# Opening of a two-layer hybrid backbone, ordered anew: filter tables first, modulation and the first wide matmuls in quarters, three units open

## The chip, the cores and the metric

The kernel runs on one NeuronCore of one Trainium2 chip. A core has five engines that work through their own instruction queues in order and wait for one another through semaphores: TensorE (PE) multiplies matrices, VectorE (DVE) and ScalarE (ACT) work elementwise, GpSimd (POOL) has next to nothing to do here, and SyncE (SP) issues the DMAs. The metric is device time in microseconds (us) of one execution.

## What is computed

A flow-matching backbone of two layers over 256 latent tokens and 256 context tokens of width 1024, all in float32. Each layer is a half-step SwiGLU, a token mixer and another half-step SwiGLU; shift, scale and gate of every sub-layer come from a modulation of the conditioning vectors. Layer 0 mixes with differential attention, layer 1 with a Hyena long convolution. What the change touches, cut from the reference:

```python
def modulation(cond, w, b):
    m = jax.nn.silu(cond) @ w + b
    return jnp.split(m[..., None, :], N_MOD, axis=-1)

def swiglu(h, wi, wo):
    a, u = jnp.split(h @ wi, 2, axis=-1)
    return (jax.nn.silu(a) * u) @ wo

def half_ffn(x, shift, scale, gate, wi, wo, g, b, alpha):
    y = swiglu(x * (1.0 + scale) + shift, wi, wo)
    return layer_norm(alpha * x + 0.5 * gate * y, g, b)

def hyena_filters(n, w1, b1, f1, w2, b2, f2, w3):   # z: 33 position features of n = 256 positions
    h = jnp.sin(f1 * (z @ w1 + b1))
    h = jnp.sin(f2 * (h @ w2 + b2))
    h = (h @ w3) * jnp.exp(-t * deltas)
    return h[:, :D_MODEL], h[:, D_MODEL:]
```

The two Hyena filters are later needed as spectra. Neither they nor the first modulation depend on the tokens, so the kernel computes them in its opening, beside the first SwiGLU.

## The kernel before

**Arithmetic.** Float32 products are made of rounded halves: a value is cast to a high half on ACT (`wH`, `xh`, `hhe`), the rest is the low half on DVE (`wL`, `xl`, `hle`), and three matmuls (high x high, high x low, low x high) replace one.

**The first SwiGLU** ("wide") takes latent and context tokens together: 512 columns. Its 22 *units* are 128 columns of the hidden width; a unit is two accumulations, `pa` and `pu`, over 8 tiles of the contraction, so 48 matmuls with 512 columns. Its weights are one 1 MB DMA (`raw<-wia`), split by `Stream._split` (L237, L238) into one of three slots (`W_BUFS`).

**The opening** is written out by hand. `START` is the order of the loads on SP's queue; `ORDER` is a list of words that `run` (L648) records one after the other, and within it every engine keeps that order (`tc.manual_schedule`). What follows it is ordered by a scheduler. The words:

- `n1`, `n2`: the two small layers of the filter net, `filter_net` (L555) with `sine` (L541: six steps on DVE, then ACT's Sin). The output is `hid1`, `hid2`.
- `t`*dt*: `filter_taps` (L575), for half d of the channels and half t of the positions: two matmuls of 64 rows (`hp`), forward and backward filter, times a decay table (`hh`).
- `ah`: split of the table of the transform. `v`*dt*: sum and difference of forward and backward taps (`heo`, L591), each split in halves.
- `s`*df*: one spectrum tile, six matmuls (`hsp`, L334) and a copy of the result by ACT (`hsb`, L607). `S`: the spectra are stored.
- `a`: `ada_unit` (L449) multiplies one 1 MB piece of the modulation weights (`rawa<-adx`) with the conditioning, four matmuls in four column strips of 32 into one psum tile (`adaps`). `F`: `ada_end` (L460) copies it (ACT, L463), transposes it (PE, `adat`) and sums it on DVE to shift and scale. `p`: `scales` (L621) adds 1 to the scale.
- `x`*j*: `modulated` (L630) scales token tile j (DVE, L633, two halves), casts the high half (ACT, L636), and leaves the low half (DVE, L628) to the next `x` or to `xl`.
- `W`: the next weights are split. `u`: `wide_unit` (L641) opens a unit and runs contraction tiles 0 to 3 of it; `g`*n* runs tiles 4 to 7 of the n-th open unit.
- `k`*n*: n filler matmuls (`warm`), which compute nothing.

Before, the modulation comes in two halves of four pieces each: `F` after the fourth and the eighth. The first half of the token tiles (`x0` to `x3`) is scaled after the first `F`, the second half after the other. Two units are opened.

**SP's queue** is strict in the opening: a load that finds no free buffer (three for `rawa`, two for `raw`) holds back all that stand behind it. A DMA also waits for the one eight places ahead of it, whose semaphore it uses again.

Of the kernel before, what the change touches and what calls it, by code (L numbers as in the profile page):

```python
# [13 lines left out]
AF = mybir.ActivationFunctionType  # L14
# [48 lines left out]
ADA_FFN = dict(b0=[2 * f for f in range(1, 9)], a1=[3 * f for f in range(1, 4)], b1=[])  # L63


START = """ah d0 a00 a01 a02 fw3 a03 w0 d2 z0 a10 z1 z2 z3 a11 d1 a12 w1 d3 a13 z4 z5 z6 z7 w2 cb""".split()

ORDER = """n1 k18 n2 k18 S a k3 t00 a ah a a W F p0 k4 t01 x0 x1 x2 x3 xl v00 k1 v01 k3 a t11 u0 a a W s01 s00
s02 a F p1 x4 x5 t10 x6 s04 x7 s03 xl u1 g0 v10 v11 g1 s10 s13 s14 s12 s11 S""".split()

RAWA_BUFS = 3
RAW_BUFS = 2
# [65 lines left out]
def lay_out(x):  # L142
    f32 = np.float32
    con = shape_constants()
    a = {}

    def put(name, arr):
        a[name] = np.ascontiguousarray(arr, dtype=f32)

    def tcols(m):  # L150
        return m.reshape(m.shape[0], KT, P).transpose(2, 1, 0)

    put("xc", np.concatenate([tcols(x["x"][0]), tcols(x["ctx"][0])], axis=2).transpose(1, 0, 2))
# [12 lines left out]
    cols(V_CB, x["hy_conv_b"][0])  # L166
    cols(V_DS, x["hy_d_skip"][0])
    cols(V_SG, x["da_subln_g"][0])
    vec[:, V_LAM:V_LAM + 256] = np.broadcast_to(x["da_lambda"].reshape(1, 256), (P, 256))
    put("cb", np.broadcast_to(np.concatenate([x["c"].reshape(D), x["c_ctx"].reshape(D)]), (P, 2 * D)))  # L170
    for i, k in enumerate(("hy_fb1", "hy_ff1", "hy_fb2", "hy_ff2")):
        vec[:64, V_F + i] = x[k][0]
    put("vec", vec)

    zf = np.zeros((64, 384), f32)
    zf[:33, 0:256] = con["z"]
    zf[:33, 256:320] = x["hy_fw1"][0]
    zf[:, 320:384] = x["hy_fw2"][0]
    put("zf", zf)
    put("fw3", x["hy_fw3"][0])  # L180
    for k in ("rope", "decay", "a_u", "a_h", "b_i", "ident"):
        put(k, con[k].reshape(P, -1))

    for i in range(2):
        w = x["ada_w"][i].reshape(KT, P, 9 * D)
        if i == 0:
            put("adx0", w[:, :, :2048].reshape(4, 2, P, 2, 2, 512).transpose(4, 0, 2, 1, 3, 5))
# [12 lines left out]
    put("who", x["hy_w_o"][0].reshape(KT, P, 4, 2, P).transpose(2, 1, 3, 0, 4))  # L200
    return a
# [108 lines left out]
def backbone(ctx, tc, A, out):  # L310
# [59 lines left out]
    for what in START:  # L370
        if what == "cb":
            items.append(dict(kind="d", src=A["cb"], dst=lambda: condb.rearrange("p q k -> p (q k)")))
        elif what[0] == "d":
            q = int(what[1])
            tload(decay, A["decay"][:, 512 * q:512 * q + 512], "tabf")
        elif what == "fw3":
            table(fw3, "tabf", A["fw3"], range(0, 2049, 512), 64)
        elif what == "ah":
            table(a_h, "tabf", A["a_h"], A_H)
        elif what[0] == "z":  # L380
            zload(int(what[1:]))
# [61 lines left out]
    mod = [cp.tile([P, 2, 72], F32, name=f"mod{i}") for i in range(2)]  # L443


    ada_first = [(h, k) for h in (0, 1) for k in range(4)]
    ada_ps = {}

    def ada_unit():  # L449

        h, k = ada_first.pop(0)
        it = st.get("a")
        if k == 0:
            ada_ps[h] = adap.tile([P, 512], F32, name="adaps", tag="ada")
        for j in range(4):
            nc.tensor.matmul(ada_ps[h][32 * j:32 * j + 32, :], condS[:, 2 * k + j // 2, :],
                             it["raw"][:, 512 * j:512 * j + 512], start=k == 0, stop=True, skip_group_check=True)
        st.done(it)

    def ada_end():  # L460
        h, ps = ada_ps.popitem()
        sb = blk("adasb")
        S.copy(sb, ps)  # L463
        pt = adap.tile([P, 512], F32, name="adat", tag="ada")
        for b in range(4):
            nc.tensor.transpose(pt[:, P * b:P * b + P], sb[:, P * b:P * b + P], ident)
        v = pt.rearrange("p (b j s) -> p s j b", b=4, j=4)

        def cols3(t, o):
            return t[:, o:o + 16].rearrange("p (j h b) -> p j h b", j=2, h=2)[:, :, h, :]  # L470

        for q in range(2):
            m3 = cols3(mod[0][:, q, :], 0)
            V.tensor_tensor(m3, v[:, q, 0:2, :], cols3(vec, V_ADAB), OP.add)
            V.tensor_tensor(m3, v[:, q, 2:4, :], m3, OP.add)

    def ada_side(n, later=ADV):

# [60 lines left out]
    C1, C2, C3 = split_2pi()  # L539

    def sine(dst, ps, bcol, fcol):  # L541
        a = blk("sa")[:64, :T]
        n = blk("sn")[:64, :T]
        V.tensor_scalar(a, ps, vec[:64, bcol:bcol + 1], vec[:64, fcol:fcol + 1], OP.add, OP.mult)
# [4 lines left out]
        V.tensor_scalar(a, a, PI_LO, -PI_LO, OP.min, OP.max)  # L549
        S.activation(dst, a, AF.Sin)  # L550
# [2 lines left out]
    ah = []  # L553

    def filter_net(n):  # L555
        ps = bank("hp")
        if n == 0:
            mm(ps[:64, :T], zf[:33, 256:320], zf[:33, 0:256], True, True)
        else:
            mm(ps[:64, :T], zf[:64, 320:384], hid[0][:64, :T], True, True)  # L560
        sine(hid[n][:64, :T], ps[:64, :T], V_F + 2 * n, V_F + 2 * n + 1)

    def table_split():
        for n, t in enumerate(a_h):
# [8 lines left out]
    raw_taps = {}  # L573

    def filter_taps(dh, tt):  # L575
        hs = []
        for g in range(2):
            ph = bank("hp3")
            mm(ph, hid[1][:64, P * tt:P * tt + P], fw3[2 * g + dh][:64, :], True, True)
            hh = blk("hh")  # L580
            V.tensor_tensor(hh, ph, decay[2 * dh + tt], OP.mult)
            if g == 1 and tt == 0:
                V.memset(hh[0:1, :], 0.0)
            hs.append(hh)
        raw_taps[dh, tt] = hs
# [32 lines left out]
    X = []  # L618
    late = []

    def scales(half):  # L621
        hs = slice(4 * half, 4 * half + 4)
        V.tensor_scalar(s1[:, :, hs], mod[0][:, :, 8 + 4 * half:12 + 4 * half], 1.0, None, OP.add)
# [24 lines left out]
    def run(what):  # L648
# [187 lines left out]
    def ffn_wide():  # L836
        nrm = Norm(Z, 512)
        for half in range(2):
# [618 lines left out]
```

## Time and profile before

| what | value |
|---|---|
| time, median of 3 runs (lowest, highest) | 1357.56 us (1355.3, 1360.0) |
| profiled execution: time, span | 1356.75 us, 1355.0 us |
| busy PE, DVE, ACT | 1310.6, 1035.4, 660.5 us |
| mean granted clock of PE | 0.975 |
| moved by DMA | 261.38 MB, mean 193 GB/s |

The profile is of one execution. In its rows, `pa<-xh,wH` names what is written and what is read, without buffer numbers; L634 or the like is the line in the kernel, and matmuls of all kinds are recorded in one helper line (L334 before). A wait in brackets names who ended it. PE's ends are modelled: matmuls follow one another faster than their durations say. A float32 matmul that isn't split shows as two PE instructions.

### The profile page before, as it was taken

What the parts mean: (1) busy time and instruction counts of PE and PEld (TensorE: products, weight loads), DVE (VectorE), ACT (ScalarE), POOL (GpSimd) and SP (SyncE); (2) the same over time, 40 slices, a digit from 0 to 9 for tenths busy, and PEclk for the clock granted to TensorE, in tenths of its full rate; (3) what the DMA queues carried; (4) which work ended last, traced back from release to release, by engine and by line L of the source; (5) the groups of instructions that cost most, each with busy time, mean ns of one, the idle gap of its engine ahead of it and who ended that gap; (6) DMA issues with size and microseconds to landing.
All of it is one profiled execution on the core that took longest, in us unless ns stands there. A gap on an engine that the chain in (4) does not pass through costs nothing.

```text
span 1355.0 us, 19282 instructions
## 1 busy us (share of the span) xinstructions
PE 1310.6 (97%) x7424; PEld 1127.2 (83%) x7424; DVE 1035.4 (76%) x1921; ACT 660.5 (49%) x1177; POOL 12.7 (1%) x12
## 2 busy tenths in 40 slices
PE   7999999999999999998999999999999999999997
PEld 4688888888888888887888888888899889888886
DVE  3899988789886777778776668766668789766664
ACT  1443322232233866665755447655446444666543
POOL 0000000000000000000000000000000110000000
PEclk8999999999998999998999998999999989899998
DMA  9967788888942212121655463654664434355452
GB/s 290 395 238 260 274 328 335 335 333 316 321 163 78 94 63 94 63 94 63 215 189 178 154 215 138 218 186 158 217 205 150 143 125 157 132 183 194 157 190 76
DMA packets 44418, 261.38 MB, mean 193 GB/s; under 512 B 4964, under 2 KB 6692, under 8 KB 19624
## 3 DMA queue, kind: packets, MB, share of 16 engines
q1 hardware_dynamic: 44328, 260.16, 53.7%
q8 instruction: 58, 0.95, 0.3%
q14 instruction: 32, 0.26, 0.1%
HBM read 256.99 MB, written 3.15 MB: 192 GB/s over the span
## 4 chain that ended last, share of the span: by engine, by line
PE 87%; DVE 7%; ACT 3%; DMA 1%; issue 1%; ACTq 0%; SPq 0%
PE py L334 24%; PE pa L334 23%; PE pu L334 23%; PE pxv L334 5%; PE pv L334 2%; DVE wL L238 2%; ACT wH L237 1%; PE hsp L334 1%; PE pka L334 1%; PE pkb L334 1%; PE warm L334 1%; PE uf L334 1%; PE lnst L334 1%; DMA raw<-wia 1%; PE po L334 1%
## 5 line engine op out<-in xcount | busy, mean ns | idle before, releaser
L238 DVE TENSOR_TENSOR wL<-raw,wH 128x1024 fp32r<-128x1024 f32 (+1 forms) x356 | 388.1, 1108 | 111.7 <-ACT wH L237 108.9
L237 ACT CAST wH<-raw 128x1024 fp32r<-128x1024 f32 (+1 forms) x356 | 329.0, 956 | 212.9 <-PE py L334 97.1
L334 PE MATMUL pa<-xhl,wH 128*128 128x512 f32 x520 | 188.7, 400 | 5.6 <-DVE xhl L813 5.6
L334 PE MATMUL pu<-xhl,wH 128*128 128x512 f32 x520 | 188.0, 398 | 0.0
L334 PE MATMUL py<-g,wH 128*128 128x512 f32 (+1 forms) x594 | 186.6, 372 | 0.0
L489 DVE SCALAR_TENSOR_TENSOR rawa<-rawa,condb 128x1024 f32<-128x1024 f32 x128 | 151.5, 1220 | 1.4 <-DMA rawa<-adr 1.1
L334 PE MATMUL py<-g,wL 128*128 128x256 f32 x528 | 147.8, 280 | 0.0
L334 PE MATMUL pa<-xhl,wL 128*128 128x256 f32 x520 | 146.6, 282 | 0.0
L334 PE MATMUL pu<-xhl,wL 128*128 128x256 f32 x520 | 146.3, 281 | 0.0
L334 PEld LDWEIGHTS py<-g,wH 128*128 128x128 f32 x594 | 107.2, 188 | 21.0
L334 PEld LDWEIGHTS pa<-xhl,wH 128*128 128x128 f32 x520 | 98.7, 190 | 29.4 <-DVE xhl L813 4.2
L334 PEld LDWEIGHTS pu<-xhl,wH 128*128 128x128 f32 x520 | 98.9, 190 | 23.3
L334 PEld LDWEIGHTS py<-g,wL 128*128 128x128 f32 x528 | 99.6, 189 | 0.1
L334 PEld LDWEIGHTS pa<-xhl,wL 128*128 128x128 f32 x520 | 99.5, 191 | 0.1
L334 PEld LDWEIGHTS pu<-xhl,wL 128*128 128x128 f32 x520 | 99.3, 191 | 0.0
L843 ACT ACTIVATE sil<-pa 128x512 f32<-128x512 f32 x22 | 13.2, 599 | 152.7 <-PE pa L334 152.7
L334 PE MATMUL pxv<-xhl,wH 128*128 128x256 f32 x384 | 73.1, 292 | 1.3 <-ACT xhl L811 1.1
L334 PE MATMUL pa<-xh,wH 128*128 128x512 f32 x176 | 68.6, 390 | 0.0
L334 PE MATMUL pa<-xh,wL 128*128 128x512 f32 x176 | 68.5, 389 | 0.0
L334 PE MATMUL pu<-xl,wH 128*128 128x512 f32 x176 | 68.5, 389 | 0.0
L334 PE MATMUL pa<-xl,wH 128*128 128x512 f32 x176 | 68.5, 389 | 0.0
L334 PE MATMUL pu<-xh,wL 128*128 128x512 f32 x176 | 68.5, 389 | 0.0
(314 smaller groups left out, 2601.8 us busy)
## 6 DMA issues: line engine op xcount, KB each, us to landing
rawa<-adr SPq DMA_DIRECT2D x64, 1024.0 KB, 7.1
raw<-wia SPq DMA_DIRECT2D x44, 1024.0 KB, 4.8
raw<-wib SPq DMA_DIRECT2D x44, 1024.0 KB, 4.8
raw<-woa SPq DMA_DIRECT2D x32, 704.0 KB, 4.2
raw<-wob SPq DMA_DIRECT2D x32, 704.0 KB, 4.1
rawa<-adx SPq DMA_DIRECT2D x8, 1024.0 KB, 9.4
raw<-wqk SPq DMA_DIRECT2D x8, 1024.0 KB, 4.8
raw<-whv SPq DMA_DIRECT2D x8, 1024.0 KB, 4.8
```

The lines of the kernel that those rows point to most:

```text
L237: nc.scalar.copy(h[:, d], it["raw"][:, s:e])
L238: nc.vector.tensor_tensor(lo[:, d], it["raw"][:, s:e], h[:, d].bitcast(F32), OP.subtract)
L334: return nc.tensor.matmul(o, l, r, start=start, stop=stop, skip_group_check=True)
L489: V.scalar_tensor_tensor(junk if q else w, w, 1.0, condb[:, q, :], OP.mult, OP.mult, accum_out=mod[i][:, q, 2 * u + h:2 * u + h + 1])
L843: S.activation(s, pa, AF.Silu)
```

## The change

- **Loads.** The filter's output weights, which were four 64-row loads, are laid out as two of 128 rows, with the forward filter on rows 0 to 63 and the backward on rows 64 to 127; the first half, two decay tables and the transform's table come first. The modulation pieces are cut differently: a quarter of the columns needs two pieces instead of half of them four.
- **Taps on both row halves.** The second filter layer writes its 64 outputs twice, on 128 partitions, and the two matmuls of `t` use different halves of PE's rows.
- **Quarters.** `F`*h* comes after every second `a`, four times in all, and is followed by the scaling of two token tiles. `g`*nh* runs two contraction tiles of open unit n; `o` opens a unit without running anything. Three units are open.
- **Scaling on ACT.** `modulated` does both halves with an ACT activation (L644 after) instead of DVE's.
- **Fillers.** 72 instructions of the first two `k` become 40; there are `k6`, `k8` and `k10` before the first wide matmul, and none after it.

The core of the diff:

```diff
-START = """ah d0 a00 a01 a02 fw3 a03 w0 d2 z0 a10 z1 z2 z3 a11 d1 a12 w1 d3 a13 z4 z5 z6 z7 w2 cb""".split()
+START = """f0 d0 d2 ah a00 a01 w0 z0 z1 a10 a11 z2 z3 w1 f1 d1 d3 a20 a21 z4 z5 w2 a30 a31 z6 z7 cb""".split()
...
-ORDER = """n1 k18 n2 k18 S a k3 t00 a ah a a W F p0 k4 t01 x0 x1 x2 x3 xl v00 k1 v01 k3 a t11 u0 a a W s01 s00
-s02 a F p1 x4 x5 t10 x6 s04 x7 s03 xl u1 g0 v10 v11 g1 s10 s13 s14 s12 s11 S""".split()
+ORDER = """n1 k10 n2 k10 ah t00 t01 a a k6 v00 F0 k8 p0 W x0 x1 xl k10 v01 o g00 s00 s01 a s02 a s03 F1 p1 s04 x2 x3 xl
+g01 W t10 t11 o g10 v10 g11 v11 a a s10 F2 p2 s11 x4 x5 xl g02 g12 s12 s13 W s14 o g20 g21 a a F3 p3 g22 x6 x7 xl
+g03 g13 g23 S""".split()
...
-    ada_first = [(h, k) for h in (0, 1) for k in range(4)]
+    ada_first = [(h, k) for h in range(4) for k in (0, 1)]
...
-            nc.tensor.matmul(ada_ps[h][32 * j:32 * j + 32, :], condS[:, 2 * k + j // 2, :],
+            nc.tensor.matmul(ada_ps[h][32 * j:32 * j + 32, :], condS[:, 4 * k + j, :],
...
         for q in range(2):
-            m3 = cols3(mod[0][:, q, :], 0)
-            V.tensor_tensor(m3, v[:, q, 0:2, :], cols3(vec, V_ADAB), OP.add)
-            V.tensor_tensor(m3, v[:, q, 2:4, :], m3, OP.add)
+            m3 = cols(mod[0][:, q, :], 0)
+            V.tensor_reduce(m3, v[:, q], AX.X, OP.add)
+            V.tensor_tensor(m3, m3, cols(vec, V_ADAB), OP.add)
...
         for g in range(2):
             ph = bank("hp3")
-            mm(ph, hid[1][:64, P * tt:P * tt + P], fw3[2 * g + dh][:64, :], True, True)
+            r = slice(64 * g, 64 * g + 64)
+            nc.tensor.matmul(ph, hid[1][r, P * tt:P * tt + P], fw3[dh][r, :], start=True, stop=True,
+                             skip_group_check=True, tile_position=(64 * g, 0))
...
         for q in range(2):
-            V.tensor_scalar(hv[:, T * q:T * q + T], Z[j][:, T * q:T * q + T], s1[:, q, j:j + 1],
-                            mcol(0, q, 0, j), OP.mult, OP.add)
+            S.activation(hv[:, T * q:T * q + T], Z[j][:, T * q:T * q + T], AF.Identity, bias=mcol(0, q, 0, j),
+                         scale=s1[:, q, j:j + 1])
...
-        elif a == "u":
+        elif a == "o":
             opened.append(wide_unit())
-            gemm(opened[-1][3], X, KT, 0, 4)
         elif a == "g":
-            gemm(opened[int(b)][3], X, KT, 4)
+            gemm(opened[int(b)][3], X, KT, 2 * int(c), 2 * int(c) + 2)
```

Where the change moves instructions, in three places. First ACT's queue around the second modulation result. Before, from the weights of the second unit on (`hsb` copies a spectrum, `adasb` the modulation, `xh` is the cast of a scaled token tile):

```order
L237 CAST wH_421<-raw_264 128x1024 x2
L607 COPY hsb_436<-hsp_429 128x512
L607 COPY hsb_445<-hsp_438 128x512
L607 COPY hsb_454<-hsp_447 128x512
L463 COPY adasb_462<-adaps_357 128x512
L636 CAST xh_477<-hv_474 128x512
L237 CAST wH_683<-raw_372 128x1024
L636 CAST xh_483<-hv_480 128x512
```

After, from the second of the first five spectra on:

```order
L619 COPY hsb_353<-hsp_346 128x512
L619 COPY hsb_375<-hsp_368 128x512
L619 COPY hsb_390<-hsp_383 128x512
L468 COPY adasb_392<-adaps_355 128x512
L619 COPY hsb_411<-hsp_404 128x512
L644 ACTIVATE hv_413<-z_222,mod0_128,s1_133 128x256 x2
L647 CAST xh_416<-hv_413 128x512
L644 ACTIVATE hv_419<-z_224,mod0_128,s1_133 128x256 x2
L647 CAST xh_422<-hv_419 128x512
L239 CAST wH_439<-raw_226 128x1024 x2
```

The scaling (`hv`) now stands on ACT itself, behind the copy of a fifth spectrum, and the next unit's weights stand behind it.

Second, PE's queue at the same place. Before, behind the last piece of the modulation:

```order
L456 MATMUL adaps_357<-rawa_362,condS_122 32x512 x4
L466 MATMUL adat_464<-ident_86,adasb_462 128x128 x4
L334 MATMUL hp3_487<-tabf_106,hid2_130 128x512
L334 MATMUL hp3_491<-tabf_110,hid2_130 128x512
L334 MATMUL hsp_503<-hhe_329,ahh_242 128x512
L334 MATMUL hsp_503<-hle_330,ahh_242 128x512
```

After, from the end of spectrum s03 to the first matmuls of the third token tile:

```order
L336 MATMUL hsp_383<-hhe_319,ahl_195 128x512
L471 MATMUL adat_394<-ident_86,adasb_392 128x128 x4
L336 MATMUL hsp_404<-hhe_249,ahh_190 128x512
L336 MATMUL hsp_404<-hle_250,ahh_190 128x512
L336 MATMUL hsp_404<-hhe_249,ahl_191 128x512
L336 MATMUL hsp_404<-hhe_313,ahh_194 128x512
L336 MATMUL hsp_404<-hle_314,ahh_194 128x512
L336 MATMUL hsp_404<-hhe_313,ahl_195 128x512
L336 MATMUL pa_323<-xh_416,wH_280 128x512
L336 MATMUL pa_323<-xl_417,wH_280 128x512
```

Between the transposition and the matmuls that need its result, PE now has one spectrum; before, it had taps, two spectra and half a unit of wide matmuls.

Third, DVE's queue at the last modulation result. Before (`heo` and `hle` are the even and odd taps):

```order
L474 TENSOR_TENSOR mod0_126<-adat_464,vec_84 128x2x4
L475 TENSOR_TENSOR mod0_126<-adat_464,mod0_126 128x2x4
L474 TENSOR_TENSOR mod0_126<-adat_464,vec_84 128x2x4
L475 TENSOR_TENSOR mod0_126<-adat_464,mod0_126 128x2x4
L623 TENSOR_SCALAR s1_131<-mod0_126 128x2x4
L633 TENSOR_SCALAR hv_474<-z_364,s1_131,mod0_126 128x256 x2
```

After, at the fourth quarter (`junk<-rawa,condb` is a side product for a later modulation):

```order
L479 TENSOR_REDUCE mod0_128<-adat_676 128x2x2
L480 TENSOR_TENSOR mod0_128<-mod0_128,vec_84 128x2x2
L494 SCALAR_TENSOR_TENSOR junk_127,mod0_128<-rawa_666,condb_81 128x1024
L634 TENSOR_SCALAR s1_133<-mod0_128 128x2x2
L494 SCALAR_TENSOR_TENSOR rawa_666,mod0_128<-rawa_666,condb_81 128x1024
L494 SCALAR_TENSOR_TENSOR junk_127,mod0_128<-rawa_666,condb_81 128x1024
L494 SCALAR_TENSOR_TENSOR rawa_666,mod0_128<-rawa_666,condb_81 128x1024
L639 TENSOR_TENSOR xl_702<-hv_698,xh_701 128x512
L639 TENSOR_TENSOR xl_708<-hv_704,xh_707 128x512
```

Side products now stand ahead of the scale's last step and ahead of the low halves of the last two token tiles.

More of the change, by code (lines that the diff above doesn't have):

```diff
@@ L171, in lay_out @@
     for i, k in enumerate(("hy_fb1", "hy_ff1", "hy_fb2", "hy_ff2")):
-        vec[:64, V_F + i] = x[k][0]
+        vec[:, V_F + i] = np.tile(x[k][0], 2)
     put("vec", vec)
-    zf = np.zeros((64, 384), f32)
+    zf = np.zeros((64, 448), f32)
     zf[:33, 0:256] = con["z"]
     zf[:33, 256:320] = x["hy_fw1"][0]
-    zf[:, 320:384] = x["hy_fw2"][0]
+    zf[:, 320:448] = np.tile(x["hy_fw2"][0], (1, 2))
     put("zf", zf)
-    put("fw3", x["hy_fw3"][0])
+    put("fw3", x["hy_fw3"][0].reshape(64, 2, D).transpose(1, 0, 2).reshape(P, D))
     for k in ("rope", "decay", "a_u", "a_h", "b_i", "ident"):
@@ L186, in lay_out @@
         if i == 0:
[L187 removed]
+            put("adx0", w[:, :, :2048].reshape(2, 4, P, 2, 4, 256).transpose(4, 0, 2, 1, 3, 5))
         put(f"adr{i}", x["ada_w"][i].T.reshape(36, 2, P, D).transpose(0, 2, 1, 3))
@@ L375, in backbone @@
             tload(decay, A["decay"][:, 512 * q:512 * q + 512], "tabf")
-        elif what == "fw3":
-            table(fw3, "tabf", A["fw3"], range(0, 2049, 512), 64)
+        elif what[0] == "f":
+            q = int(what[1])
+            tload(fw3, A["fw3"][:, 512 * q:512 * q + 512], "tabf")
         elif what == "ah":
@@ L416, in backbone @@
     st = Stream(nc, tc, rawp, rawap, wsp, blk, items, strict)
-    zf = blk("zf")[:64, :384]
+    zf = blk("zf")[:64, :448]
     nc.sync.dma_start(zf, A["zf"])
@@ L455, in ada_unit, with ada_end @@
         for j in range(4):
-            nc.tensor.matmul(ada_ps[h][32 * j:32 * j + 32, :], condS[:, 2 * k + j // 2, :],
+            nc.tensor.matmul(ada_ps[h][32 * j:32 * j + 32, :], condS[:, 4 * k + j, :],
                              it["raw"][:, 512 * j:512 * j + 512], start=k == 0, stop=True, skip_group_check=True)
         st.done(it)
-    def ada_end():
-        h, ps = ada_ps.popitem()
+    def ada_end(h):
+        ps = ada_ps.pop(h)
         sb = blk("adasb")
@@ L466, in ada_end, with cols @@
             nc.tensor.transpose(pt[:, P * b:P * b + P], sb[:, P * b:P * b + P], ident)
-        v = pt.rearrange("p (b j s) -> p s j b", b=4, j=4)
-        def cols3(t, o):
-            return t[:, o:o + 16].rearrange("p (j h b) -> p j h b", j=2, h=2)[:, :, h, :]
+        v = pt.rearrange("p (m b j s) -> p s m b j", m=2, b=2, j=4)
+        def cols(t, o):
+            return t[:, o:o + 16].rearrange("p (m h b) -> p m h b", m=2, h=4)[:, :, h, :]
         for q in range(2):
-            m3 = cols3(mod[0][:, q, :], 0)
-            V.tensor_tensor(m3, v[:, q, 0:2, :], cols3(vec, V_ADAB), OP.add)
-            V.tensor_tensor(m3, v[:, q, 2:4, :], m3, OP.add)
+            m3 = cols(mod[0][:, q, :], 0)
+            V.tensor_reduce(m3, v[:, q], AX.X, OP.add)
+            V.tensor_tensor(m3, m3, cols(vec, V_ADAB), OP.add)
     def ada_side(n, later=ADV):
@@ L541, in sine @@
     def sine(dst, ps, bcol, fcol):
-        a = blk("sa")[:64, :T]
-        n = blk("sn")[:64, :T]
-        V.tensor_scalar(a, ps, vec[:64, bcol:bcol + 1], vec[:64, fcol:fcol + 1], OP.add, OP.mult)
+        r = ps.shape[0]
+        a = blk("sa")[:r, :T]
+        n = blk("sn")[:r, :T]
+        V.tensor_scalar(a, ps, vec[:r, bcol:bcol + 1], vec[:r, fcol:fcol + 1], OP.add, OP.mult)
         V.tensor_scalar(n, a, 1.0 / TWO_PI, MAGIC, OP.mult, OP.add)
@@ L556, in filter_net @@
         ps = bank("hp")
+        r = 64 * (n + 1)
         if n == 0:
-            mm(ps[:64, :T], zf[:33, 256:320], zf[:33, 0:256], True, True)
+            mm(ps[:r, :T], zf[:33, 256:320], zf[:33, 0:256], True, True)
         else:
-            mm(ps[:64, :T], zf[:64, 320:384], hid[0][:64, :T], True, True)
-        sine(hid[n][:64, :T], ps[:64, :T], V_F + 2 * n, V_F + 2 * n + 1)
+            mm(ps[:r, :T], zf[:64, 320:448], hid[0][:64, :T], True, True)
+        sine(hid[n][:r, :T], ps[:r, :T], V_F + 2 * n, V_F + 2 * n + 1)
     def table_split():
@@ L575, in filter_taps @@
     def filter_taps(dh, tt):
-        hs = []
+        hs, phs = [], []
         for g in range(2):
             ph = bank("hp3")
-            mm(ph, hid[1][:64, P * tt:P * tt + P], fw3[2 * g + dh][:64, :], True, True)
+            r = slice(64 * g, 64 * g + 64)
+            nc.tensor.matmul(ph, hid[1][r, P * tt:P * tt + P], fw3[dh][r, :], start=True, stop=True,
+                             skip_group_check=True, tile_position=(64 * g, 0))
+            phs.append(ph)
+        for g, ph in enumerate(phs):
             hh = blk("hh")
@@ L619, in backbone, with scales @@
     late = []
-    def scales(half):
-        hs = slice(4 * half, 4 * half + 4)
-        V.tensor_scalar(s1[:, :, hs], mod[0][:, :, 8 + 4 * half:12 + 4 * half], 1.0, None, OP.add)
+    def scales(h):
+        V.tensor_scalar(s1[:, :, 2 * h:2 * h + 2], mod[0][:, :, 8 + 2 * h:10 + 2 * h], 1.0, None, OP.add)
     def low():
@@ L667, in run @@
         elif a == "F":
-            ada_end()
+            ada_end(int(b))
         elif a == "W":
@@ L856, in ffn_wide @@
             if half == 0:
-                done = sum(w[0] == "g" for w in ORDER)
                 for it, pa, pu, outs in opened:
-                    if f >= done:
-                        gemm(outs, X, KT, 4)
                     st.done(it)
```

## Prediction

> **What bounds the kernel now.** I read the page first: what share TensorE (PE) has, and who holds the chain that ended last.
>
> ```profile
> span 1355.0 us, 19282 instructions
> PE 1310.6 (97%) x7424; PEld 1127.2 (83%) x7424; DVE 1035.4 (76%) x1921; ACT 660.5 (49%) x1177; POOL 12.7 (1%) x12
> PE 87%; DVE 7%; ACT 3%; DMA 1%; issue 1%; ACTq 0%; SPq 0%
> ```
>
> PE sets the end, and the change touches only the opening, so next came the opening in windows (length, busy us of PE, its weight loads, DVE, ACT and POOL, granted clock, DMA share, GB/s), and then the chain of waits in order of time over the first 60 us (start, us, what).
>
> ```profile
> 0.00:10.00 10.00, 6.81 (x30) 6.05 (x31) 4.17 (x24) 1.92 (x3) 0.20 (x4) 1.00 0.74 195
> 10.00:20.00 10.00, 7.75 (x62) 6.10 (x61) 2.64 (x7) 1.84 (x5) 0.00 (x0) 1.00 1.04 327
> 20.00:30.00 10.00, 8.57 (x28) 2.10 (x28) 3.55 (x8) 1.22 (x2) 0.00 (x0) 0.50 0.90 301
> 90.00:100.00 10.00, 10.00 (x46) 8.29 (x45) 10.00 (x18) 3.53 (x5) 0.00 (x0) 1.00 0.86 283
> ```
>
> ```profile
> 11.68 4.21 PE warm L334 x36
> ...
> 17.32 11.44 DMA raw<-wia
> ...
> 38.77 0.89 PE pa L334 x3
> ...
> 44.43 1.85 PE adaps L456 x16
> 46.29 4.35 PE hsp L334 x18
> 50.63 1.04 PE adaps L456 x8
> ...
> 51.70 0.59 ACT adasb L463
> ...
> 52.34 0.66 PE adat L466 x4
> 52.99 1.91 PE hp L334 x4
> ```
>
> Until 38.7 us PE does fillers (warm), filter work and modulation, and waits for DMA (11.44 us for the first weights); between 20 and 30 us it has half its clock. From 38.7 it works through. The last wait of the opening is the 0.59 us copy at 51.70. Afterwards PE is full: 10.00 of 10 in the window at 90 us. So the change is worth what it does to one moment: when PE takes up the fourth wide unit, with all filter spectra done.
>
> ```profile
> 57.69 0.39 PE L334 MATMUL pa<-xh,wH 128*128 128x512 f32 x1
> 91.79 0.39 PE L334 MATMUL pa<-xh,wH 128*128 128x512 f32 x1
> ```
>
> In the PE timeline that is 91.79. Between these rows lie 120 wide and 30 spectrum matmuls, 34.10 us, so one takes 0.227 at full clock.
>
> **The change, part by part.** All is costed against the profiled execution: 1356.75 us, of which 1355.0 is the span; the median of the runs, 1357.56, is 0.8 higher.
>
> *Earlier start.* Rows for the ScalarE (ACT) and VectorE (DVE) steps:
>
> ```profile
> 8.40 0.42 ACT L550 ACTIVATE hid<-sa 64x256 f32<-64x256 f32 x1 [2.11 <-DVE sa L549]
> 11.72 0.54 DVE L544 TENSOR_SCALAR sa<-hp,vec 64x256 f32<-64x256 f32 x1 [3.35 <-PE hp L334]
> 14.60 0.42 ACT L550 ACTIVATE hid<-sa 64x256 f32<-64x256 f32 x1 [5.78 <-DVE sa L549]
> 26.07 0.48 DVE L583 MEMSET hh<- 1x512 f32 x1 [0.16 <-DVE hh L581]
> 26.48 1.61 DVE L508 TENSOR_TENSOR ahl<-tabf,ahh 128x384 fp32r<-128x384 f32 x4
> 40.72 0.68 DVE L591 TENSOR_TENSOR heo<-hh 128x512 f32<-128x512 f32 x1
> 42.70 0.69 DVE L591 TENSOR_TENSOR heo<-hh 128x512 f32<-128x512 f32 x1
> 48.70 1.28 DVE L581 TENSOR_TENSOR hh<-hp,tabf 128x512 f32<-128x512 f32 x2
> 49.90 2.35 DVE L238 TENSOR_TENSOR wL<-raw,wH 128x1024 fp32r<-128x1024 f32 x2
> 53.70 0.17 DVE L623 TENSOR_SCALAR s<-mod 128x8 f32<-128x8 f32 x1
> 432.35 1.09 ACT L811 ACTIVATE xh<-z,lnp 128x256 fp32r<-128x256 f32 x2 [1.55 <-DVE z L805]
> 47.44 0.62 ACT L507 CAST hhe<-heo 128x512 fp32r<-128x512 f32 x1 [1.42 <-DVE heo L591]
> 49.87 1.55 ACT L607 COPY hsb<-hsp 128x512 f32<-128x512 f32 x3
> ```
>
> The second filter layer no longer stands behind 36 filler instructions (20 now): the first layer's sine is done at 8.82, a matmul of about 1.1 at half clock follows, then the same DVE and ACT steps (11.72 to 15.02, 3.3), so hid2 is there at about 13.35 instead of 15.02. The half tables on 128 partitions land before it. DVE then does the table splits (1.6, started with ACT's), four tap products and the memset (4 x 0.61 + 0.5 = 3.0), and two even/odd rounds, one each 1.98 (40.72 to 42.70). ACT's copy of the modulation psum stands behind the second round's cast, so it ends at 22.1, and DMA is no longer what it waits for: at the windows' 195, 327 and 301 GB/s the 5.6 MB up to the second z tile are there at about 21. Transposes 0.66 and five small DVE operations of 0.17 give 23.9. Scaling is now two ACT operations in 1.09 (L811 has the same form) and a 0.62 cast: 25.7. PE gets there later, at 26.9, after 36 filler instructions of 0.117 (4.21 / 36). **That is 11.8 before the 38.7 of now.** The wait for DMA is gone; what is late instead is DVE's queue, ahead of ACT's copy. The scaling leaves DVE (16 operations of 0.4), which has no part in the next sum.
>
> *Work still to do from there.* Now: 204 matmuls 46.3, three modulation units 2.9, one transposition 0.7, one tap pair 1.9, waits and gaps 1.3: 53.0. After: 46.3, six units 5.6, three transpositions 2.0, taps 1.9: 55.8. Without any wait, PE would be at the fourth unit at 82.7, 9.1 early.
>
> *New waits.* The work now comes in four quarters, and each quarter's scaling needs a round trip PE, ACT, PE, DVE, ACT, DVE, for which PE has only one spectrum (1.4 us) as cover. On ACT the order is spectrum copy, modulation copy, spectrum copy, scaling. Durations are those above. From the end of a matmul's 0.227 slot to ACT it takes another 0.2: the row of 57.69 lasts 0.39, and 0.04 is the handover.
>
> 1. Second quarter, transposes: 0.2 + 0.5 (copy of s03, ahead) + 0.58 + 0.05 = 1.3.
> 2. Its scaling: the copy of s04 lets it start 0.7 after s04. The first tile's cast ends 1.74 later (1.09 + 0.62 + handover), the second's 3.39; DVE's low half takes 0.72 more, 4.11, and five of the second tile's six matmuls come behind that. PE is through after 0.7 + 4.11 + 1.14 = 5.95, of which 12 matmuls are 2.72: 3.2 of waiting.
> 3. s10 needs the third even/odd round; DVE has the split of the second weights (2.35), tap products 3.0 and three rounds 6.0 ahead of it: 0.5.
> 4. Third quarter, transposes behind the fourth round's cast: 1.65.
> 5. Its scaling: as 2, but the conditioning's Silu stands between scaling and cast of the second tile (ACT row below, 1.91): 5.0.
> 6. The third unit's weights are split by ACT behind s13's copy: PE is there after s14, 1.36 later; cast 1.05 and first low half 1.22, second the same: 1.7.
> 7. Fourth quarter: transposes 0.75; DVE's side products (row below, 1.22 each) stand once ahead of the scale and three times ahead of the low half: 3.5.
>
> ```profile
> 57.68 1.91 ACT L690 ACTIVATE condb<-condb 128x2048 f32<-128x2048 f32 x1
> L489 DVE SCALAR_TENSOR_TENSOR junk<-rawa,condb 128x1024 f32<-128x1024 f32 x9 | 10.9, 1216 | 0.0
> raw<-wib SPq DMA_DIRECT2D x44, 1024.0 KB, 4.8
> ```
>
> Sum 17.6: the fourth unit at 82.7 + 17.6 = 100.3, **8.5 later** than 91.79. Who waits behind a waiting instruction is in each case PE's whole queue, since it has one order.
>
> *Row halves.* No row here shows two 64-row matmuls side by side. If each pair takes one matmul's time, t10 and t11 take 1.9; if two, 3.8, and 1.9 is added (the first pair of pairs lies under DVE's 1.6 + 3.0). I take side by side, since 16 modulation instructions of 512 columns in four column strips took 1.85, against 1.91 for 4 of 512 columns in the tap rows. The Trainium skill (TensorE: Matmul & The Clock Gate, Part 3: Packing small matmuls) says that tiles in different row groups overlap; no run here shows it yet.
>
> *SP's queue.* Its order is strict: behind the sixth modulation load, which waits until PE has used the third, stand z4, z5 and the third weights; behind the eighth, which waits for PE's fifth, stand z6, z7, cb and the first side load. A 1 MB load alone takes 4.8 (row above), so cb is there 4.8 + 4 x 0.65 + 1.3 = 8.7 after PE's fifth, and ACT wants it about 9 after. The ten spectrum stores now go behind all of it; their cover is that nobody reads them until hyena.
>
> *Clock.* Windows of 3.41 us, the step in which the granted clock changes:
>
> ```profile
> 16.52:19.93 3.41, 1.23 (x10) 0.74 (x6) 0.00 (x0) 0.00 (x0) 0.00 (x0) 1.00 1.08 188
> 19.93:23.34 3.41, 1.91 (x3) 0.85 (x4) 0.00 (x0) 0.00 (x0) 0.00 (x0) 0.50 0.95 250
> 467.07:470.49 3.42, 1.97 (x11) 0.90 (x9) 3.36 (x7) 3.39 (x6) 0.00 (x0) 1.00 0.19 79
> 470.49:477.31 6.82, 6.82 (x18) 3.97 (x17) 6.39 (x15) 5.08 (x12) 0.00 (x0) 0.50 0.01 4
> 589.95:593.37 3.42, 2.01 (x18) 2.04 (x19) 3.42 (x12) 3.36 (x9) 0.00 (x0) 1.00 0.38 153
> 593.37:596.78 3.41, 3.41 (x32) 3.41 (x31) 3.41 (x7) 2.06 (x5) 0.00 (x0) 1.00 0.00 0
> ```
>
> A window with 1.97 busy was followed by half clock, one with 2.01 was not: about 1.4 us idle within a window is enough. After has four such places: about 3 us idle before the first transposes (PE is through with fillers at 19), then waits 1 and 2, 4 and 5, 7. Each costs half of 3.4 to 6.8 us of PE work, partly under the wait itself: 2.0 each, estimated, 8 in all (nothing to 14). The Trainium skill (the same page, Why this matters for your kernels) asks only that PE not be idle for more than about 3 us between bursts. By that rule waits 1 to 7 cost no clock, and the sum ends at 8.5; the window at 467.07 speaks against it.
>
> So 8.5 + 8 = 16.5; 1356.75 + 16.5 is **1373**.
>
> **Rivals.** (a) The waits come, the clock stays: +8.5, 1365. For it: 589.95 kept its clock. Against: 467.07. (b) Faster: the round trips are covered. Kept are the 9.1; a sum of waits of 4 leaves 1352. For it: DVE is free of 16 scalings, and the start is 11.8 earlier; against: ACT's order, in which the scaling stands behind a copy of the spectrum that PE has just finished. It decides at waits plus clock of 9.1. (c) Waits plus clock just eat the start: within 4 us of now, which is 0.3% and about what a measurement of this kernel can tell from no change. (d) cb and the first side load come late, since the fourth quarter's last load waits for PE: wait 5 and wait 6 grow by up to 5, 1378 to 1382. For it: a margin of 0.3; against: DMA is otherwise idle there. (e) The row halves run one after the other: +1.9, 1375.
>
> **How the numbers follow.** Forecast with clock loss 0.58, with (e) inside it; (a) 0.2; (d) 0.07; (b) 0.08; (c) 0.07. Range 1360 to 1383: down to a sum of waits of 12 with no clock loss, up to (d) or 14 of clock loss; it leaves out (b) and most of (c). Faster 0.08, same 0.07, slower 0.85.
>
> **What would show it.** In after: hid2 near 13.4, first wide matmul between 26 and 30, the fourth unit's first matmul near 100 to 109; PE idle before adat and before pa<-xh,wH with ACT as releaser, about 17 us in all; half clock in four stretches of the first 110 us. Wrong would be a fourth unit before 92, or a loss that arises after it, where I cost the change at nothing because PE is full.

## The result, and the profile after

| | kernel before | changed kernel |
|---|---|---|
| time, median (lowest, highest) | 1358.74 us (1355.3, 1360.0), 4 runs | 1367.88 us (1365.74, 1370.11), 4 runs |
| ratio, 95% interval | | 1.0071 (1.0045 to 1.0098) |
| profiled execution: time, span | 1356.75, 1355.0 | 1370.11, 1368.3 |

It is slower by 0.7%. In another comparison (after_again, below) the same kernel came out at 1.0097 (1.0063 to 1.0131). First the head of the page of after, its first chain row, and the windows that were shown of before:

```profile
span 1368.3 us, 19284 instructions
PE 1311.2 (96%) x7426; PEld 1126.1 (82%) x7426; DVE 1031.8 (75%) x1915; ACT 670.9 (49%) x1195; POOL 13.1 (1%) x12
PE 78%; DVE 11%; ACT 5%; DMA 3%; issue 1%; ACTq 0%; SPq 0%; DVEq 0%
```

```profile
0.00:10.00 10.00, 6.77 (x26) 5.36 (x27) 4.30 (x25) 1.92 (x3) 0.20 (x4) 1.00 0.75 214
10.00:20.00 10.00, 7.84 (x56) 4.48 (x55) 8.07 (x18) 2.46 (x6) 0.00 (x0) 1.00 1.02 421
20.00:30.00 10.00, 7.90 (x48) 7.62 (x49) 7.29 (x15) 6.84 (x11) 0.00 (x0) 0.83 1.03 409
90.00:100.00 10.00, 7.06 (x23) 5.11 (x22) 8.40 (x14) 5.62 (x9) 0.00 (x0) 0.83 1.02 363
```

PE is busy for 1311.2 us, nearly as before (1310.6); so 12.7 of the 13.3 that the span grew are idle time. The opening did become denser between 10 and 30 us: DMA moves 409 to 421 GB/s there instead of 327 and 301. But at 90 us, where PE was full before, it is busy for 7.06 of 10.

PE's timeline of after shows where the idle time lies. The rows with a bracket are the main ones that waited; the first and the last row are the first wide matmul and the first of the fourth unit.

```profile
28.17 0.48 PE L336 MATMUL pa<-xh,wH 128*128 128x512 f32 x1
...
40.21 0.66 PE L471 MATMUL adat<-ident,adasb 128*128 128x128 f32 x4 [1.16 <-ACT adasb L468]
...
44.56 0.50 PE L336 MATMUL pa<-xh,wH 128*128 128x512 f32 x1 [2.31 <-ACT xh L647]
45.28 0.50 PE L336 MATMUL pa<-xl,wH 128*128 128x512 f32 x1 [0.22 <-DVE xl L639]
...
60.74 0.66 PE L471 MATMUL adat<-ident,adasb 128*128 128x128 f32 x4 [1.31 <-ACT adasb L468]
...
65.11 0.50 PE L336 MATMUL pa<-xh,wH 128*128 128x512 f32 x1 [2.31 <-ACT xh L647]
...
68.41 0.50 PE L336 MATMUL pa<-xh,wH 128*128 128x512 f32 x1 [1.15 <-ACT xh L647]
...
78.89 0.50 PE L336 MATMUL pa<-xh,wL 128*128 128x512 f32 x1 [0.53 <-DVE wL L240]
...
91.64 0.50 PE L336 MATMUL pa<-xh,wH 128*128 128x512 f32 x1 [1.01 <-ACT xh L647]
94.06 0.50 PE L336 MATMUL pa<-xl,wH 128*128 128x512 f32 x1 [1.92 <-DVE xl L639]
...
103.73 0.39 PE L336 MATMUL pa<-xh,wH 128*128 128x512 f32 x1
```

The first wide matmul is 10.5 earlier than the 38.70 of before, the fourth unit 11.94 later than the 91.79. At the second half's first matmul of a later stage (`py<-gh,wH`, 190.77 against 178.83) the distance is still 11.94, and the span ends 13.3 longer. So nine tenths of the loss lie ahead of the fourth unit.

Why PE waits is seen on the other two engines. ACT at the second and third quarter, then DVE at the fourth (two views of after):

```profile
42.28 0.59 ACT L619 COPY hsb<-hsp 128x512 f32<-128x512 f32 x1 [2.12 <-PE hsp L336]
42.77 1.09 ACT L644 ACTIVATE hv<-z,mod,s 128x256 f32<-128x256 f32 x2
43.89 0.62 ACT L647 CAST xh<-hv 128x512 fp32r<-128x512 f32 x1
...
64.96 1.09 ACT L644 ACTIVATE hv<-z,mod,s 128x256 f32<-128x256 f32 x2
65.96 1.90 ACT L700 ACTIVATE condb<-condb 128x2048 f32<-128x2048 f32 x1
67.76 0.60 ACT L647 CAST xh<-hv 128x512 fp32r<-128x512 f32 x1
```

```profile
88.50 1.22 DVE L494 SCALAR_TENSOR_TENSOR junk<-rawa,condb 128x1024 f32<-128x1024 f32 x1
...
89.64 0.17 DVE L634 TENSOR_SCALAR s<-mod 128x4 f32<-128x4 f32 x1
...
92.17 1.22 DVE L494 SCALAR_TENSOR_TENSOR rawa<-rawa,condb 128x1024 f32<-128x1024 f32 x1
...
93.33 1.29 DVE L639 TENSOR_TENSOR xl<-hv,xh 128x512 fp32r<-128x512 f32 x2
```

At 42.28 ACT has stood idle for 2.12 us, waiting for PE's last cover, the spectrum whose copy stands ahead of the scaling. PE, through with it, waits 2.31 for the cast that ends at 44.51. At 65.96 the Silu stands between scaling and cast. At 88.50 DVE does side products while PE needs the scale and the low halves.

### The profile page after: what moved, and what is told of

Same layout as the page of the kernel before. It is cut to its first block, busy times and chain, and to the rows that moved or that the text cites. A ratio compares the mean times of both kernels' runs of the same rounds, so it can differ in the third digit from the quotient of the medians.

```text
span 1368.3 us, 19284 instructions
## 1 busy us (share of the span) xinstructions
PE 1311.2 (96%) x7426; PEld 1126.1 (82%) x7426; DVE 1031.8 (75%) x1915; ACT 670.9 (49%) x1195; POOL 13.1 (1%) x12
## 4 chain that ended last, share of the span: by engine, by line
PE 78%; DVE 11%; ACT 5%; DMA 3%; issue 1%; ACTq 0%; SPq 0%; DVEq 0%
PE pa L336 22%; PE pu L336 22%; PE py L336 20%; PE pxv L336 4%; DVE wL L240 3%; PE pv L336 2%; ACT wH L239 2%; DMA raw<-woa 1%; PE pkb L336 1%; PE pka L336 1%; PE hsp L336 1%; PE lnst L336 1%; PE warm L336 1%; PE po L336 1%; PE sc L1059 1%
```

## The experiments

All were compared with the kernel before, on their own chip; "ratio" is against it, with the 95% interval. "Fourth unit" is the start of its first matmul in the profiled execution (91.79 before, 103.73 after). For the waits, the bracket of each waiting row was taken, and what the modelled end of the matmul ahead lies beyond its 0.227 slot (0.16, or 0.27 where that matmul had waited itself); the prediction had counted them so. In after they sum to 16.26. The expectations of cover, dve_scale, late_side and clock count from a fourth unit of after at about 104.9 (cover's says so, and the sums of the others come out with it); it is at 103.73, so their moments are about 1.2 too late. Theory: these waits are the loss. Rivals: the scaling's place on ACT by itself, the clock, and a loss that arises behind the opening.

**1. Cover for the round trips (cover).** The loads, the quarters and the scaling on ACT stay; words move, and the modulation copy gets a word of its own, C:

```diff
-... k6 v00 F0 k8 p0 W x0 x1 xl k10 v01 o g00 s00 s01 a s02 a s03 F1 p1 s04 x2 x3 xl
-g01 W t10 t11 o g10 v10 g11 v11 a a s10 F2 p2 s11 x4 x5 xl g02 g12 s12 s13 W s14 o g20 g21 a a F3 p3 g22 x6 x7 xl
+... k6 v00 C0 F0 k8 p0 W x0 x1 xl k10 v01 o g00 W a a C1 t10 s00 t11 s01 F1 p1
+x2 x3 xl s02 s03 v10 s04 g01 v11 a a C2 o g10 F2 p2 x4 x5 xl W g11 s10 s11 a a C3 g02 F3 p3 x6 x7 xl g12 s12 s13 s14
```

> Same loads, quarters, fillers ahead of the first wide matmul and ScalarE scaling as the changed kernel; only the order of the words after the first quarter differs, and the modulation copy is a word of its own (C) ahead of the transposes (F). Each quarter's pieces are multiplied one stage earlier, its copy stands ahead of the spectrum copies on ScalarE, and behind its transposes PE has 4 to 7 us of spectra or of another unit's tiles instead of 1.4. Theory (the quarters' round trips are uncovered): PE works through from 28.2; 55.8 us of work plus a remainder of 0 to 4 us of waits puts the fourth unit's first matmul at 84 to 88, 17 to 21 earlier than the 104.9 of the changed kernel, and the time at 1347 to 1351, below the kernel before. Rival (scaling on ScalarE itself is what costs, its 16 operations of 0.55 us): they are all still there, so at least 8 of the 13 us lost stay, 1363 or more. Rival (the clock): at most the two half-clock windows go, 1.7 each, 1364 to 1368. Rival (the loss arises behind the opening): 1368 whatever the opening does.

Measured: 1351.3 us against 1355.88, ratio 0.996 (0.9938 to 0.9982). PE's timeline of cover, from the first wide matmul to the fourth unit; the row in the middle is the only wait of more than half a microsecond:

```profile
27.47 0.47 PE L336 MATMUL pa<-xh,wH 128*128 128x512 f32 x1
...
37.46 0.60 PE L474 MATMUL adat<-ident,adasb 128*128 128x128 f32 x4
...
50.84 0.66 PE L474 MATMUL adat<-ident,adasb 128*128 128x128 f32 x4 [1.11 <-ACT adasb L468]
...
85.65 0.39 PE L336 MATMUL pa<-xh,wH 128*128 128x512 f32 x1
```

The waits fell from 16.26 to 1.53 and the fourth unit came 18.1 earlier, as the theory had it, of which the waits are 14.7 (the time is 0.3 above the range that it gave); the order alone turns the change from 0.7% slower to 0.4% faster. All 16 scaling operations are still on ACT, so their place is not what costs, and nothing behind the opening holds the loss.

**2. ACT's order alone (act_order).** The same division of F, and the scaling's words ahead of a spectrum that stood ahead of them; PE's queue is that of the changed kernel, instruction for instruction.

```diff
-... s02 a s03 F1 p1 s04 x2 x3 xl
+... s02 a C1 s03 F1 p1 x2 x3 xl s04
-... a a s10 F2 p2 s11 x4 x5 xl
+... a a C2 s10 F2 p2 x4 x5 xl s11
```

> The changed kernel with PE's queue unchanged, instruction for instruction; only ScalarE's queue differs in the second and third quarter: the modulation copy stands ahead of the spectrum copy that PE has not reached yet, the scaling of both token tiles ahead of the next one, and the Silu ends up behind the casts. Theory (the loss is made of two things, copies ahead of the scaling on ScalarE and too little PE work as cover): the first kind goes, about 1.3 in the second quarter's transposes, 1.4 in its scaling, 1 and 1.8 in the third quarter: 5 together, fourth unit at 98.7, 5 us faster than the changed kernel, still slower than the kernel before. Rival (order on ScalarE is all of it): fourth unit at 90 or less. Rival (cover is all of it): fourth unit at 102 to 104.

Measured: 1364.71 us, ratio 1.0052 (1.0032 to 1.0072), beside the changed kernel's 1371.14 on this chip: 6.4 less. The fourth unit stands at 101.24. The waits sum to 10.73, 5.53 less (5 expected). The fourth unit is 2.5 later than expected: half clock followed three of the waits, in after only one.

```profile
42.60 0.49 PE L336 MATMUL pa<-xh,wH 128*128 128x512 f32 x1 [1.33 <-ACT xh L650]
...
62.98 0.50 PE L336 MATMUL pa<-xh,wH 128*128 128x512 f32 x1 [1.36 <-ACT xh L650]
```

Both scaling waits shrink from 2.31 to about 1.35, what the round trip takes by itself with one spectrum as cover, and the transposes of the second quarter no longer wait. So a third of the waits was ACT's order. Of the other 10.73, the fourth quarter's 4.2 are in part DVE's side products, as late_side (6) shows; the rest is put down to missing cover on PE, which cover bears out, though it moved other words as well.

**3. The changed kernel once more (after_again).**

> The changed kernel once more, on the chip of the three runs beside it, so that they can be compared with it and not only with the kernel before. Every theory: 0.5 to 1.0 per cent slower than the kernel before, the fourth unit's first matmul between 102 and 105.

Measured: 1371.14 us, ratio 1.0097 (1.0063 to 1.0131); fourth unit at 106.35, outside what was expected: half clock took 4.8 more than in after (below).

**4. Scaling back on DVE (dve_scale),** L644 as before the change.

```diff
-            S.activation(hv[...], Z[j][...], AF.Identity, bias=mcol(0, q, 0, j), scale=s1[:, q, j:j + 1])
+            V.tensor_scalar(hv[...], Z[j][...], s1[:, q, j:j + 1], mcol(0, q, 0, j), OP.mult, OP.add)
```

> The changed kernel with the scaling back on VectorE (two operations of 0.4 us for a token tile). Theory: the scaling no longer stands behind a spectrum copy; the second wait shrinks by 1.1, the fifth by 2.8 (the Silu then stands behind both casts), the seventh grows by 1.5, because the scaling now stands among VectorE's side products: fourth unit at 102.5, time 1365 to 1366. Rival (scaling on ScalarE is the cause of the loss): fourth unit at 92, time 1355 to 1359.

Measured: 1365.83 us, ratio 1.0068 (1.0049 to 1.0087), fourth unit at 100.37. The waits sum to 13.64, 2.62 less than in after (2.4 expected), but against the kernel before no difference from the changed kernel can be told.

**5. The same in the covered order (cover_dve).**

> The covered order of the run before (cover) with the scaling back on VectorE. Theory: with 4 to 7 us of PE work behind each transposition nobody waits for the scaling, wherever it is done; within 2 us of cover, 0.2 to 0.6 per cent faster than the kernel before. Rival (ScalarE is the better place, since it leaves VectorE free): 3 us or more slower than cover. Rival (VectorE is the better place): 3 us or more faster than cover.

Measured: 1350.44 us, ratio 0.9949 (0.9929 to 0.9969); fourth unit at 86.01 against 85.65. With cover, no difference between the two places of the scaling can be told.

**6. Later modulation out of the opening (late_side).**

```diff
         for what in ORDER:
             run(what)
+        S.activation(condb, condb, AF.Silu)
     st.hold = False
     st.pump()
-    S.activation(condb, condb, AF.Silu)
```

> The changed kernel with the conditioning's Silu put behind the last token tile's cast on ScalarE, so that VectorE's side products come after the opening too. Theory: the fifth wait loses the 1.9 us Silu between scaling and cast (1.5 less), the seventh the four 1.27 us side products (2.7 less), and with them the half-clock window at 94.8 goes (1.7): fourth unit at 99, time 1362. Rival (scaling on ScalarE itself): nothing of it has moved, 1367 to 1368. Rival (side products pushed out come back as waits later): fourth unit at 99 too, but time 1365 or more.

Measured: 1372.7 us, ratio 1.0112 (1.0086 to 1.0139): a miss of the theory's time. The fourth unit did come earlier, at 100.06, with waits of 11.61, 4.65 less; 2.9 of that is the seventh wait, where the side products had stood. Two half-clock windows (from 45.85 and from 66.33), for the one of after, took a part of the gain. But then PE waits for the fourth unit's low weights, which on DVE stand behind the side products that were pushed out. PE and DVE of late_side:

```profile
100.06 0.39 PE L336 MATMUL pa<-xh,wH 128*128 128x512 f32 x1
107.37 0.79 PE L336 MATMUL pa<-xh,wL 128*128 128x512 f32 x1 [5.34 <-DVE wL L240]
```

```profile
104.95 1.22 DVE L494 SCALAR_TENSOR_TENSOR junk<-rawa,condb 128x1024 f32<-128x1024 f32 x1
...
106.09 1.22 DVE L240 TENSOR_TENSOR wL<-raw,wH 128x1024 fp32r<-128x1024 f32 x1
```

The third expectation, that they come back as waits later, is what happened. The raw buffer came free late with it: ACT's next cast waits 11.35 for its load, until 115.82.

**7. Fillers where PE waits (clock).** 14 more `k` ahead of the first transposes and 6 fewer behind, and 8 between `pa<-xh,wH` and `pa<-xl,wH` of the seventh token tile.

```diff
-... a a k6 v00 F0 k8 p0 W x0 x1 xl k10 v01 ...
+... a a k20 v00 F0 k12 p0 W x0 x1 xl v01 ...
...
+                    mm(t, h, X[6][0], False, False)
+                    if n == 0:
+                        run("k8")
+                    mm(t, h, X[6][1], False, False)
```

> The changed kernel with fillers put where PE waits, to hold its clock: 14 more of them ahead of the first transposes and 6 fewer behind, and 8 between the first matmul of the seventh token tile and the one that waits 1.9 us for its low half. Theory (waits, little clock): no half-clock window in the first 110 us any more; the first wide matmul about 1.5 earlier, of which the next spectrum gives back half a microsecond, and 1.7 less around 95: fourth unit at 102, time 1365. Rival (the clock costs the 8 us that the prediction gave it): fourth unit at 97, time 1360.

Measured: 1368.62 us, ratio 1.0079 (1.0051 to 1.0107); first wide matmul at 26.08, fourth unit at 102.32. The two half-clock windows of after are gone, but a new one has come behind the second quarter's wait, where no filler had been put, and the 1.4 gained at the fourth unit is less than the intervals of the times can tell.

**8. The first quarter in the covered order too (cover2).** On top of cover: C0, F0 and the scaling ahead of the even and odd taps, and `v`*ds* for one sign of both halves (two `heo`, then two casts, then two `hle`).

```diff
-... t00 t01 a a k6 v00 C0 F0 k8 p0 W x0 x1 xl k10 v01 o g00 W a a C1 t10 s00 t11 s01 F1 p1
-x2 x3 xl s02 s03 v10 s04 g01 v11 ...
+... t00 t01 a a C0 k3 F0 p0 W x0 x1 xl k16 v00 o g00 v01 a a C1 s00 s01 F1 p1 W x2 x3 xl s04
+s02 s03 t10 t11 g01 v10 v11 ...
```

> The covered order with the first quarter treated alike: its modulation copy, transposes and scaling ahead of the even and odd taps on ScalarE and VectorE, which come sign by sign behind the first two token tiles. Theory: the first wide matmul follows the first weights (landed at 18.8 in cover, split in 2.0, scaling 1.1, cast 0.6): 22.7 instead of 27.5; of these 4.8 us the spectra give some back, since their taps are ready later; fourth unit at 79 to 82 (85.7 in cover, 91.8 before), 3 to 6 us faster than cover, 0.7 to 0.9 per cent faster than the kernel before. Rival (the loads hold it back now, as the third and fourth quarter's pieces must land earlier): fourth unit at 84 or later, as cover.

Measured: 1347.3 us against 1357.17, ratio 0.9918 (0.9886 to 0.995). PE's timeline of cover2:

```profile
22.57 0.49 PE L336 MATMUL pa<-xh,wH 128*128 128x512 f32 x1 [0.20 <-ACT xh L651]
...
37.55 1.61 PE L591 MATMUL hp<-tabf,hid 64*128 64x512 f32 x4 [0.72 <-ACT hsb L623]
...
81.58 0.39 PE L336 MATMUL pa<-xh,wH 128*128 128x512 f32 x1
```

Both moments are as worked out (22.7; 79 to 82). The spectra gave back only 0.8 of the 4.9.

**9. Spectra ahead of the wide matmuls (spec_first), beside cover2 once more (cover2_again).**

```diff
-... C0 k3 F0 p0 W x0 x1 xl k16 v00 o g00 v01 a a C1 s00 s01 F1 p1 W x2 x3 xl s04
-s02 s03 t10 t11 g01 v10 v11 ...
+... C0 k3 F0 p0 v00 k14 v01 W x0 x1 xl s00 s01 s04 a a C1 s02 s03 F1 p1 o g00 x2 x3 xl
+t10 t11 g01 W v10 v11 ...
```

> As cover2, but the first five spectra go ahead of the first wide matmul, behind the first quarter's transposes: the wide work starts at about 31 instead of 22.6, with two quarters of the modulation done, so that the first quarter's early scaling is of no use by itself. Theory (what counts is how long PE has nothing to do between 22 and the fourth unit, not when the wide work starts): PE's spectra start at 22.2, the sum of PE's work is the same, the fourth unit stands at 80 to 83 as in cover2 (81.6) and the time is within 2 us of it. Rival (the early first wide matmul is what gains): the fourth unit 5 us or more later than in cover2, the time near that of cover (0.4 per cent faster than the kernel before).

> cover2 once more, beside spec_first on the same chip. Both theories: 0.6 to 1.1 per cent faster than the kernel before, fourth unit at 81 to 83.

Measured: 1346.35 us, ratio 0.9922 (0.9893 to 0.9952), beside 1345.74, ratio 0.9919 (0.9893 to 0.9945), with the fourth unit of cover2_again at 81.19. PE's timeline of spec_first, first spectrum, first wide matmul and fourth unit:

```profile
21.82 0.48 PE L336 MATMUL hsp<-hhe,ahh 128*128 128x512 f32 x1
...
31.86 0.48 PE L336 MATMUL pa<-xh,wH 128*128 128x512 f32 x1
...
82.22 0.39 PE L336 MATMUL pa<-xh,wH 128*128 128x512 f32 x1
```

The wide work starts 9.3 later, and in time nothing is lost that can be told. So what counts is when PE gets lasting work of any kind, here at 21.82 and in cover2 at 22.57, less what it waits afterwards. The fourth unit is 1.0 later than in cover2_again, because the transposes of the second quarter wait here:

```profile
47.38 0.66 PE L474 MATMUL adat<-ident,adasb 128*128 128x128 f32 x4 [2.81 <-ACT adasb L468]
```

Which single wait costs what, taken away one at a time, was not tried, and neither was what half as many quarters would give.

## Why the prediction was right, and where its terms were off

The direction, the place of the loss and its mechanism came as forecast: 1367.88 measured (1370.11 profiled), 1373 predicted, within the range. The change itself was forecast at +16.5; it was +9.1 by the medians, +13.4 between the two profiled executions, and +14.0 in the other comparison. Rival (a), the same waits without clock loss, gave 1365, and 1367.88 lies nearer to that than to 1373; only the clock term is between the two. The terms by their own steps, up to the fourth unit, in two executions of the changed kernel:

| term | predicted | after | after_again |
|---|---|---|---|
| first wide matmul | 26.9 | 28.17 | 27.91 |
| work from there | 55.8 | 57.8 | 57.2 |
| seven waits | 17.6 | 16.3 | 14.9 |
| half clock from there | 8 in all, the first place included | 1.55 | 6.3 |
| fourth unit | 108.3 | 103.73 | 106.35 |

Half clock is summed from start to start of PE's instructions: a matmul in a half-clock window counts 0.227 as work and the rest as clock. Work is what then remains of the way to the fourth unit. That the sum is off by only 4.6 and 2.0 is in part luck: the work was set too low, while the waits and, in after, the clock were set too high.

*Earlier start: right.* The second sine ended at 13.22 (13.35 predicted), ACT's modulation copy at 22.05 (22.1), the first cast at 25.58 (25.7). PE came 1.3 late because the 36 filler instructions took 5.57, from their start to the first wide matmul, instead of 4.21, most of it at half clock; that belongs to the clock term.

*Row halves: right.* PE's timeline shows, first before, then after, that both tap pairs, four matmuls of 64 rows and 512 columns, now take the time that one pair had taken on the same rows (a matmul is two PE instructions here):

```profile
52.92 1.98 PE L334 MATMUL hp<-tabf,hid 64*128 64x512 f32 x4
...
13.27 1.99 PE L588 MATMUL hp<-tabf,hid 64*128 64x512 f32 x8 [1.02 <-ACT hid L556]
```

This is the overlap that the Trainium skill (TensorE: Matmul & The Clock Gate, Part 3: Packing small matmuls) states for tiles in different row groups; this case now shows it.

*New waits: right.* One by one, predicted and measured: 1.3 and 1.3; 3.2 and 3.0; 0.5 and 0; 1.65 and 1.5; 5.0 and 4.8; 1.7 and 1.5; 4.25 and 4.2. The Silu stood where it was expected, and its load was not waited for, so rival (d) did not come. In cover and act_order the waits shrink and the loss with them, so they are the loss and not only beside it.

*Work from there: 55.8 was 1.4 to 2.0 too small.* Matmuls behind a wait follow one another at up to 0.34 instead of 0.227 at first, and two modulation pieces that stand apart take more than two together.

*Clock: the step that failed, in its size.* I took four places at 2.0 each. In after only the first and the last lost the clock: 1.4 ahead of the first wide matmul (the fillers) and 1.55 behind wait 7, 2.9 together. In after_again all four did: 1.3 and 6.3, 7.6 together. The same waits lie differently in the windows of 3.41 us, which do not begin with the program. The window pairs at waits 2 and 5 in after, and then those of after_again with the window behind each:

```profile
40.19:43.60 3.41, 2.03 (x10) 1.44 (x10) 0.76 (x5) 1.32 (x3) 0.00 (x0) 1.00 1.04 435
43.60:47.02 3.42, 2.24 (x8) 1.32 (x8) 1.39 (x2) 3.36 (x7) 0.00 (x0) 1.00 0.48 201
60.67:64.08 3.41, 2.05 (x10) 1.44 (x10) 0.76 (x5) 1.27 (x4) 0.00 (x0) 1.00 1.03 418
64.08:67.50 3.42, 1.93 (x6) 1.05 (x6) 0.69 (x1) 3.39 (x5) 0.00 (x0) 1.00 1.02 426
```

```profile
42.76:46.17 3.41, 1.60 (x6) 1.12 (x7) 0.89 (x2) 3.35 (x7) 0.00 (x0) 1.00 0.68 286
46.17:49.58 3.41, 3.41 (x10) 2.10 (x10) 2.86 (x3) 1.67 (x2) 0.00 (x0) 0.50 0.00 0
63.24:66.65 3.41, 1.09 (x4) 0.36 (x2) 0.63 (x2) 2.75 (x6) 0.00 (x0) 1.00 1.06 441
66.65:70.06 3.41, 3.11 (x7) 1.78 (x6) 0.80 (x2) 2.75 (x3) 0.00 (x0) 0.50 1.01 423
```

In after, a window's edge (43.60, 64.08) falls into each wait of 2.3; both sides keep 1.9 to 2.2 busy and the clock stays. In after_again most of the first wait and all of the second lie inside one window, which is left with 1.60 and 1.09 busy, and the next has half the clock. That the place in the window decides is argued, and it isn't the whole rule. In clock, 1.91 of the third quarter's wait of 2.31 lie in one window, against 1.58 of the first wait in after_again; that window is left with 1.50 busy, and the next keeps its clock:

```profile
61.37:64.78 3.41, 1.50 (x8) 0.91 (x6) 0.76 (x5) 1.84 (x4) 0.00 (x0) 1.00 1.05 424
64.78:68.19 3.41, 1.95 (x6) 1.04 (x6) 0.69 (x1) 3.41 (x5) 0.00 (x0) 1.00 1.00 420
```

Of the eight waits of 2.3 in after, after_again, late_side and clock, half clock followed five. So a wait of 2.3 has a chance of costing clock, not a price, and my 8 should have been a range with its middle near 5. The prediction's step from one window with 1.97 busy and one with 2.01 to "about 1.4 us idle within a window is enough" was too much for two rows. The Trainium skill (the same page, What's actually happening) says that the window is free-running and isn't reset at a kernel's start; the trace agrees, since the edges, counted from the program's first instruction, lie 0.85 apart in the two executions. The Trainium skill's advice to leave no idle gap above about 3 us (the same page, Why this matters for your kernels) was not enough here: gaps of 2.3 were followed by half clock.

*Behind the fourth unit* I costed nothing. The distance to before is 11.94 at the fourth unit, then 10.0 at one later stage (642.97 against 632.97), 13.7 at another (1033.22 against 1019.50), and 13.3 at the end. The half-clock windows explain a part. Up to the first of these stages before has one more of them (470.49 to 477.31, where after has 483.93 to 487.34), which is 1.7 of the 1.9 that the distance shrank. From there to the second, after is in half clock for 3.2 us more (from 1030.05), a loss of 1.6, but the distance grew by 3.7; where the other 2.1 come from stays open.

The rival on the other side (faster: the round trips are covered) named the right condition, and cover and cover2 are the kernels that meet it.

## What to carry to other kernels

When work is cut into smaller pieces to start earlier, count the round trip of each piece through the other engines (here about 5 us: in cover 0.6 for the modulation copy and 4.0 from the transposes at 37.46 to the end of the first low half) and put that much independent PE work between asking and needing; the same instructions in another order were 18 us apart at the fourth unit. In an in-order queue, nothing that still waits for a later step may stand ahead of the step that is waited for. An early start of one kind of work is worth nothing by itself as long as PE has other work to do: with the first wide matmul at 22.57 or at 31.86 the time was the same.

## What the runs showed of the hardware

- Two executions of one program differ by 2.6 us at the fourth unit, because half clock took 1.55 behind the first wide matmul in one and 6.3 in the other. The 3.41 us windows of the granted clock lie 0.85 us apart in them.
- How busy a window must be to keep the clock was not found: 1.50 kept it in clock, 1.84 in act_order (40.83 to 44.24) and 1.97 in before did not. In before even a window shown as busy throughout (419.29 to 422.70, mostly matmuls of one column) was followed by half clock. The busy time that the profile shows does not separate them.
- Two 64-row matmuls on different row halves cost what one of them costs: 1.99 us for four in after, where before two on the same rows took 1.98.
